# The up- and down-projection stages of a two-layer encoder: both down-projection units of a tile placed behind the third chain of sums

## The chip, the cores and the metric

The kernel runs on one core of a Trainium2 chip. The time is the device time of one execution in microseconds; a median of three executions is given, and one further execution was profiled. TensorE (PE in the profile) does the matrix products, with its weight loads shown apart as PEld; ScalarE (ACT) copies, casts and applies activation functions; VectorE (DVE) adds, subtracts and multiplies; GpSimd (POOL) and SyncE (SP) mostly issue transfers here.

## What is computed

The reference is a trunk of two layers on 512 tokens of width 1024. What matters here is the second half of each layer, the gated channel mixer with a causal convolution of width 3:

```python
def conv_ffn(h, w_up, conv_w, conv_b, w_down):
    u, g = jnp.split(h @ w_up, 2, axis=-1)
    g = causal_dwconv(g, conv_w, conv_b)
    return (jax.nn.silu(g) * u) @ w_down
...
x = x + conv_ffn(rmsnorm(x, norm_ffn_g[l]), ffn_w_up[l], ffn_conv_w[l], ffn_conv_b[l], ffn_w_down[l])
```

The hidden width is 2816, so the up-projection has 2 x 2816 columns (a part `u` and a part `g`), and the down-projection sums over 2816 rows. All of it is in float32.

## The kernel before

**Precision.** Every float32 operand is split into a high and a low part (`split`: a cast on ACT gives the high part, a subtraction on DVE the low one), and a product is three matmuls, high by high, high by low, low by high (`mm3`, lines 194 to 196). A chain is twelve such matmuls into one PSUM tile (four slices of the inner dimension).

**Tiles.** The mixer goes over 22 tiles `j` of 128 hidden columns. The first five (`plain`) are done as ordinary projections. Tiles 5 to 21 go through `later`, one call of `step` a tile; this loop runs once in each layer, and the change is inside `step`. There the `u` and `g` columns of a tile form a 2 x 2 block matrix whose product is taken with seven block products instead of eight (a Strassen-Winograd scheme). So a step has seven chains of matmuls 256 columns wide: a11, a12, s2, s1, s3, a22 and s4 in the order of the letters used below. The chains a11, s2, s3 and a22 add up in one PSUM tile `r1`, and after each of the four ACT copies the running sum out (`A.copy`, lines 842 and 834). The next chain into `r1` may not start before that copy is done. a12 goes to `r2`; s1 and s4 go to `r3`, whose half-way value DVE reads at line 857 before s4 may be added.

**Down-projection units.** The down-projection is cut into 32 units of twelve matmuls 512 columns wide (four hidden tiles into 128 output columns; `down_products`). A table `UNITS` says which units stand in which step: none in step 21, one in steps 5 to 8 (the second place), two in steps 9 to 20. I call the two places d0 and d1. After a unit, `add_down` copies its PSUM tile out on ACT (line 777) and a POOL transfer adds it to the sum in memory (line 778).

**Work for the neighbours.** Beside its own products a step finishes the tile before it (`Tail`: `last_block` at line 938, the convolution's taps at lines 692 and 685, Silu at line 950, the gate product at line 953, the split into hidden parts) and prepares the weights of the tile after it (`Forms`: sums and differences of weight blocks at line 888, and splits of them, each an ACT cast and a DVE subtraction at lines 140 and 141). `split_up`, `split_sums` and `split_down` split tiles of 1024 columns (into `wh`/`wl`), the others of 512 (into `fh`/`fl`).

**What sets the order.** Inside the loop PE, ACT and DVE run exactly in the order in which `step` is written (`manual_schedule`); each engine takes its instructions in order, so an instruction that waits holds up all that stands behind it on its engine. Loads on SP and transfers on POOL wait for buffers.

Of the kernel before, what the change touches and what calls it, by code (L numbers as in the profile page):

```python
# [46 lines left out]
H = S // 2  # L47
# [7 lines left out]
def trunk(  # L55
# [34 lines left out]
    def sb(tag, shape, dtype=F32):  # L90
        count[0] += 1
        return pool.tile(shape, dtype, tag=tag, name=f"{tag}{count[0]}", bufs=bufs[tag])

    def ps(tag):
        count[0] += 1
        return psum.tile([P, S], F32, tag=tag, name=f"p{tag}{count[0]}", bufs=pbufs[tag])
# [179 lines left out]
    class Norm:  # L276


        def __init__(self):
            self.acc = self.row = None  # L280
# [166 lines left out]
    with tc.manual_schedule(engines={mybir.EngineType.PE, mybir.EngineType.Activation, mybir.EngineType.DVE}):  # L447

        w = ps("mm")
# [215 lines left out]
    class ChannelMixer:  # L665
# [100 lines left out]
        def down_products(self, u):  # L766
            g, j = divmod(u, KT)
            w = self.down[u // 2]
            o = ps("tr")
            c = slice(u % 2 * P, (u % 2 + 1) * P)  # L770
            for k in range(GROUP):
                mm3(o, w[0][:, k, c], w[1][:, k, c], *self.hid[GROUP * g + k], k == 0, k == GROUP - 1)
            return j, o
# [52 lines left out]
        def step(self, j, w, nxt, tail):  # L826
            def then(o, *names):
                for name in names if o is not None else ():
                    getattr(o, name)()

            def sum_products(o, r, w, i):

                self.products(r, w, self.t(i))
                A.copy(o, r[:, :H])

            new = Tail(self, j)
            then(tail, "last_block", "first_tap")
            w.split_fourth()
            r1, r2, new.r3 = ps("mm"), ps("mm"), ps("sc")
            new.up, new.u3, new.pre = sb("t", [P, S]), sb("t", [P, S]), sb("t", [P, S])  # L840
            self.products(r1, w.a11, self.b(0, 0), True)
            A.copy(new.up[:, :H], r1[:, :H])
            then(tail, "second_tap")
            self.products(r2, w.a12, self.b(1, 0), True)
            V.tensor_tensor(out=new.up[:, :H], in0=new.up[:, :H], in1=r2[:, :H], op=ALU.add)
            then(tail, "third_tap")
            sum_products(new.up[:, H:], r1, w.s2, 2)
            then(nxt, "sums")
            then(tail, "gated")
            then(nxt, "split_second", "sum_third")  # L850
            w.down_products(0)
            self.products(new.r3, w.s1, self.t(1), True)
            w.add_down(0)
            then(tail, "split")
            then(nxt, "split_up")
            sum_products(new.u3[:, :H], r1, w.s3, 3)
            V.tensor_tensor(out=new.pre[:, H:], in0=new.u3[:, :H], in1=new.r3[:, :H], op=ALU.add)
            then(nxt, "split_sums")
            w.down_products(1)
            then(nxt, "sum_fourth")  # L860
            w.add_down(1)
            sum_products(new.pre[:, :H], r1, w.a22, 4)
            then(nxt, "split_down", "split_gate")
            self.products(new.r3, w.s4, self.b(1, 1))
            return new, nxt

    class Forms:


        def __init__(self, mixer, j):  # L870
            self.mixer = mixer
            self.units = UNITS.get(j, (None, None))
            self.up, self.gate = mixer.load_pair(j)
            self.raw_down = {u // 2: mixer.load_down(u // 2) for u in self.units if u is not None and u % 2 == 0}
            self.s13 = mixer.s[:, :D].rearrange("p (a b) -> p a b", a=KT)
            self.s24 = mixer.s[:, D : 2 * D].rearrange("p (a b) -> p a b", a=KT)
# [44 lines left out]

        def down_products(self, i):
            if self.units[i] is not None:
                self.o = self.mixer.down_products(self.units[i])

        def add_down(self, i):
            if self.units[i] is not None:
                self.mixer.add(*self.o)

    class Tail:  # L930

# [373 lines left out]
    def blocks(pt, o, step, n):  # L1305
        a = pt[:, o : o + P]
        return bass.AP(tensor=a.tensor, offset=a.offset, ap=[list(a.ap[0]), [step, n], [1, P]])
# [230 lines left out]
```

## Time and profile before

| | |
|---|---|
| median of 3 runs | 1180.85 us (1180.72 to 1180.89) |
| profiled execution, its own time | 1181.04 us |
| its span, first to last instruction | 1179.3 us |
| granted TensorE clock | 0.999 |
| one-unit step (steps 5 to 8), from one a11 to the next | about 12.3 us |
| two-unit step (steps 9 to 20) | about 15.0 us |

The page gives for each engine the time in which it was busy and its share of the span. Rows of a timeline start with the start time and the duration in microseconds; a bracket at the end gives the idle time of the engine before the instruction and what ended it. Rows of matmuls overlap, since matmuls are pipelined: what one costs is the distance from its start to the start of the next.

### The profile page before, as it was taken

How to read it: one execution, taken by the hardware profiler on the slowest of the kernel's cores; microseconds unless marked ns; L12 is line 12 of the kernel's file. 1: busy time of each engine (PE TensorE's matmuls, PEld its weight loads, DVE VectorE, ACT ScalarE, POOL GpSimd, SP SyncE). 2: the span in 40 equal slices, each digit the busy share in tenths (PEclk: the TensorE clock that was granted, in tenths of full speed). 3: DMA queues.
4: the chain of work that ended last, by engine and by line, in shares of the span. 5: the costliest groups of instructions: out<-in, count | busy, mean ns of one | idle time of the engine just before them, and what ended most of it. 6: DMA issues, size and time to landing. Idle time of an engine off the chain costs nothing.

```text
span 1179.3 us, 18676 instructions
## 1 busy us (share of the span) xinstructions
PE 1169.1 (99%) x7007; PEld 1034.2 (88%) x7007; DVE 935.7 (79%) x1688; ACT 725.8 (62%) x1294; POOL 129.9 (11%) x222
## 2 busy tenths in 40 slices
PE   9999999999999999999999999999999999999997
PEld 9988888888889999999888888888889999999986
DVE  6877788887978877777698888897897877777755
ACT  6548677654655655555666667776565655555545
POOL 1111101000021111111020000101001011111100
PEclk9999999999999999999999999999999999999999
DMA  8645325244266677765564312335426466666551
GB/s 299 208 109 134 94 55 152 76 139 121 90 166 163 164 164 162 164 148 129 150 200 125 90 54 85 106 102 177 139 90 153 108 143 144 143 143 141 123 158 72
DMA packets 200156, 158.64 MB, mean 135 GB/s; under 512 B 8344, under 2 KB 179838, under 8 KB 200066
## 3 DMA queue, kind: packets, MB, share of 16 engines
q1 hardware_dynamic: 183906, 119.74, 34.6%
q0 software_dynamic: 15584, 36.67, 16.4%
q8 instruction: 55, 0.90, 0.3%
q10 hardware_dynamic: 576, 1.05, 0.2%
q14 instruction: 35, 0.29, 0.1%
HBM read 128.89 MB, written 32.46 MB: 137 GB/s over the span
## 4 chain that ended last, share of the span: by engine, by line
PE 94%; DVE 3%; ACT 1%; issue 0%; DMA 0%; SPq 0%; POOL 0%; ACTq 0%; POOLq 0%; DVEq 0%
PE pmm L194 18%; PE pmm L195 18%; PE pmm L196 18%; PE ptr L195 6%; PE ptr L194 6%; PE ptr L196 6%; PE psc L195 5%; PE psc L196 5%; PE psc L194 5%; PE psc L544 2%; PE ptr L1365 1%; PE ptr L1386 1%; PE ptr L1387 1%; PE ptr L627 1%; PE ptr L613 0%; DVE pt L141 0%
## 5 line engine op out<-in xcount | busy, mean ns | idle before, releaser
L194 PE MATMUL pmm<-u,wh 128*128 128x512 f32 (+1 forms) x968 | 333.2, 345 | 0.4 <-ACT u L140 0.2
L196 PE MATMUL pmm<-u,wl 128*128 128x512 f32 (+1 forms) x968 | 330.8, 342 | 0.0
L195 PE MATMUL pmm<-u,wh 128*128 128x512 f32 (+1 forms) x968 | 330.5, 342 | 0.0
L141 DVE TENSOR_TENSOR wl<-wr,wh 128x1024 fp32r<-128x1024 f32 (+3 forms) x172 | 199.6, 1162 | 101.8 <-ACT wh L140 101.4
L140 ACT CAST wh<-wr 128x1024 fp32r<-128x1024 f32 (+3 forms) x172 | 172.0, 1002 | 92.7 <-PE pmm L195 39.0
L196 PEld LDWEIGHTS pmm<-u,wl 128*128 128x128 f32 x968 | 181.9, 188 | 20.6
L194 PEld LDWEIGHTS pmm<-u,wh 128*128 128x128 f32 x968 | 181.8, 188 | 19.3 <-ACT u L140 1.1
L195 PEld LDWEIGHTS pmm<-u,wh 128*128 128x128 f32 x968 | 182.0, 188 | 18.5 <-DVE u L141 0.5
L194 PE MATMUL ptr<-u,wh 128*128 128x512 f32 x272 | 106.7, 392 | 0.0
L195 PE MATMUL ptr<-u,wh 128*128 128x512 f32 x272 | 106.5, 392 | 0.0
L196 PE MATMUL ptr<-u,wl 128*128 128x512 f32 x272 | 105.8, 389 | 0.0
L778 POOL DMA_DIRECT2D xspill<-t x64 | 55.6, 869 | 447.3 <-ACT t L777 437.5
L141 DVE TENSOR_TENSOR fl<-pt,fh 128x512 fp32r<-128x512 f32 x102 | 70.3, 689 | 11.2 <-ACT fh L140 8.5
L194 PE MATMUL pmm<-u,fh 128*128 128x256 f32 x272 | 75.4, 277 | 0.0
L195 PE MATMUL pmm<-u,fh 128*128 128x256 f32 x272 | 75.2, 276 | 0.0
L196 PE MATMUL pmm<-u,fl 128*128 128x256 f32 x272 | 75.2, 276 | 0.0
L195 PE MATMUL psc<-u,wh 128*128 128x256 f32 (+1 forms) x232 | 75.1, 324 | 0.0
L196 PE MATMUL psc<-u,wl 128*128 128x256 f32 (+1 forms) x232 | 75.1, 324 | 0.0
L194 PE MATMUL psc<-u,wh 128*128 128x256 f32 (+1 forms) x232 | 75.0, 324 | 0.0
L140 ACT CAST fh<-pt 128x512 fp32r<-128x512 f32 x102 | 62.7, 615 | 13.5 <-DVE pt L888 13.3
L950 ACT ACTIVATE t<-t 128x512 f32<-128x512 f32 x34 | 21.5, 632 | 79.2 <-DVE t L685 79.2
L777 ACT COPY t<-ptr 128x512 f32<-128x512 f32 x64 | 37.6, 587 | 51.6 <-PE ptr L196 51.6
(335 smaller groups left out, 2540.3 us busy)
## 6 DMA issues: line engine op xcount, KB each, us to landing
wr<-in_ffn_w_up_dram SPq DMA_DIRECT2D x54, 512.0 KB, 5.0
wr<-in_ffn_w_down_dram SPq DMA_DIRECT2D x38, 512.0 KB, 4.1
pt<-in_ffn_w_up_dram SPq DMA_DIRECT2D x34, 512.0 KB, 6.9
xspill<-t POOLq DMA_DIRECT2D x64, 256.0 KB, 4.7
wr<-in_a_w_in_dram SPq DMA_DIRECT2D x20, 512.0 KB, 3.8
wr<-in_w_kv_dram SPq DMA_DIRECT2D x12, 512.0 KB, 4.0
xspill<-fh POOLq DMA_DIRECT2D x16, 256.0 KB, 2.6
xspill<-fl POOLq DMA_DIRECT2D x16, 256.0 KB, 3.0
```

Source lines behind the costliest of these rows:

```text
L140: high = A.copy(hi, src) if on_act else V.tensor_copy(hi, src)
L141: low = V.tensor_tensor(out=lo, in0=src, in1=f(hi), op=ALU.subtract)
L194: nc.tensor.matmul(o, lh, rh, start=first, stop=False, skip_group_check=more)
L195: nc.tensor.matmul(o, lh, rl, start=False, stop=False, skip_group_check=more)
L196: nc.tensor.matmul(o, ll, rh, start=False, stop=last, skip_group_check=more)
L544: nc.tensor.matmul(o, a, b, start=first and i == 0, stop=i == 1)
L627: nc.tensor.matmul(o2, vs[a][:, 2 * hp + h, :], p[h][:, a, :], start=i == 0, stop=i == 3)
L777: A.copy(t, o)
L778: G.dma_start(xspill[j], t, accum_op=ALU.add)
L950: A.activation(self.acc, self.acc, AF.Silu)
L1365: nc.tensor.transpose(tp[:, b * P : (b + 1) * P], es[T, h][:, b * P : (b + 1) * P], ident)
L1386: nc.tensor.matmul(o2[:, s * P :], w, hi_at(pts[h], s, s, TT - s), start=s == 0, stop=False)
```

## The change

Only the order inside `step` changes. On PE the chains of a two-unit step stood as a11, a12, s2, **d0**, s1, s3, **d1**, a22, s4; now they stand as a11, a12, s2, s1, s3, **d0, d1**, a22, s4. Since both units' PSUM tiles are now held at once, `self.o` becomes a dictionary with an entry for each. The ACT and DVE work is written in a new order around this:

```diff
-            then(tail, "second_tap")
+            then(tail, "second_tap", "third_tap")
             self.products(r2, w.a12, self.b(1, 0), True)
             V.tensor_tensor(out=new.up[:, :H], in0=new.up[:, :H], in1=r2[:, :H], op=ALU.add)
-            then(tail, "third_tap")
             sum_products(new.up[:, H:], r1, w.s2, 2)
             then(nxt, "sums")
+            self.products(new.r3, w.s1, self.t(1), True)
             then(tail, "gated")
             then(nxt, "split_second", "sum_third")
-            w.down_products(0)
-            self.products(new.r3, w.s1, self.t(1), True)
-            w.add_down(0)
+            sum_products(new.u3[:, :H], r1, w.s3, 3)
             then(tail, "split")
             then(nxt, "split_up")
-            sum_products(new.u3[:, :H], r1, w.s3, 3)
             V.tensor_tensor(out=new.pre[:, H:], in0=new.u3[:, :H], in1=new.r3[:, :H], op=ALU.add)
-            then(nxt, "split_sums")
+            w.down_products(0)
             w.down_products(1)
-            then(nxt, "sum_fourth")
+            then(nxt, "split_sums", "sum_fourth")
+            w.add_down(0)
+            then(nxt, "split_gate")
             w.add_down(1)
+            then(nxt, "split_down")
             sum_products(new.pre[:, :H], r1, w.a22, 4)
-            then(nxt, "split_down", "split_gate")
             self.products(new.r3, w.s4, self.b(1, 1))
...
-                self.o = self.mixer.down_products(self.units[i])
+                self.o[i] = self.mixer.down_products(self.units[i])
...
-                self.mixer.add(*self.o)
+                self.mixer.add(*self.o[i])
```

On PE, in step 12 of the first layer, the end of the unit d0 (`ptr891`) and what stands behind it, before: the chain s1 (`psc885`).

```order
L195 MATMUL ptr891_4770<-u786_4099,wh2874_4679 128x512
L196 MATMUL ptr891_4770<-u785_4098,wl2875_4680 128x512
L194 MATMUL psc885_4716<-u640_3275,wh1870_4645 128x256
L195 MATMUL psc885_4716<-u640_3275,wh1870_4645 128x256
L196 MATMUL psc885_4716<-u640_3275,wl1871_4646 128x256
```

The same place of the same step now: d0 is `ptr895`, and the second unit `ptr896` follows at once.

```order
L195 MATMUL ptr895_4804<-u785_4111,wh2876_4670 128x512
L196 MATMUL ptr895_4804<-u785_4111,wl2877_4671 128x512
L194 MATMUL ptr896_4817<-u680_3454,wh2876_4670 128x512
L195 MATMUL ptr896_4817<-u681_3455,wh2876_4670 128x512
L196 MATMUL ptr896_4817<-u680_3454,wl2877_4671 128x512
```

Between a unit and a chain of 256 columns PE now changes width twice in such a step, where it did so four times.

On ACT, from Silu of the tile before (line 950) to the last splits of the step, before. `t886` is the tile's `up`, `t887` its `u3`, `t888` its `pre`; `wh0` is `split_up`, `wh1` `split_sums`, `wh2` `split_down`, `fh889` `split_second`, `fh903` `split_gate`.

```order
L950 ACTIVATE t880_4708<-t880_4708 128x512
L834 COPY t886_4717<-pmm883_4714 128x256
L140 CAST fh889_4765<-pt633_3237 128x512
L777 COPY t892_4795<-ptr891_4770 128x512
L140 CAST u893_4798<-t880_4708 128x512
L140 CAST wh0895_4802<-wr878_4703 128x1024
L834 COPY t887_4718<-pmm883_4714 128x256
L140 CAST wh1897_4820<-pt633_3237 128x1024
L777 COPY t900_4838<-ptr899_4824 128x512
L834 COPY t888_4719<-pmm883_4714 128x256
L140 CAST wh2901_4854<-wr879_4705 128x1024
L140 CAST fh903_4858<-pt632_3236 128x512
```

The same stretch of ACT now (`fh900` is `split_gate`):

```order
L950 ACTIVATE t880_4708<-t880_4708 128x512
L834 COPY t886_4717<-pmm883_4714 128x256
L140 CAST fh889_4777<-pt633_3237 128x512
L834 COPY t887_4718<-pmm883_4714 128x256
L140 CAST u891_4795<-t880_4708 128x512
L140 CAST wh0893_4799<-wr878_4703 128x1024
L140 CAST wh1897_4830<-pt633_3237 128x1024
L777 COPY t899_4835<-ptr895_4804 128x512
L140 CAST fh900_4838<-pt632_3236 128x512
L777 COPY t902_4842<-ptr896_4817 128x512
L140 CAST wh2903_4845<-wr879_4705 128x1024
L834 COPY t888_4719<-pmm883_4714 128x256
```

The copy of `u3` has moved ahead of the casts of the hidden tile and of `split_up`; `split_gate` and `split_down` have moved ahead of the copy of `pre`.

On DVE, from `split_down` of the step before to the first sum of weight blocks, before:

```order
L141 TENSOR_TENSOR wl2875_4680<-wr852_4530,wh2874_4679 128x1024
L141 TENSOR_TENSOR fl877_4684<-pt632_3236,fh876_4683 128x512
L938 TENSOR_TENSOR t859_4542<-t859_4542,psc858_4541 128x256
L141 TENSOR_TENSOR fl882_4711<-pt633_3237,fh881_4710 128x512
L685 SCALAR_TENSOR_TENSOR t880_4708<-t861_4544,cols1_799,t880_4708 128x511
L845 TENSOR_TENSOR t886_4717<-t886_4717,pmm884_4715 128x256
L685 SCALAR_TENSOR_TENSOR t880_4708<-t861_4544,cols1_799,t880_4708 128x510
```

The same seven instructions now:

```order
L141 TENSOR_TENSOR fl874_4664<-pt632_3236,fh873_4663 128x512
L141 TENSOR_TENSOR wl2877_4671<-wr852_4530,wh2876_4670 128x1024
L938 TENSOR_TENSOR t859_4542<-t859_4542,psc858_4541 128x256
L141 TENSOR_TENSOR fl882_4711<-pt633_3237,fh881_4710 128x512
L685 SCALAR_TENSOR_TENSOR t880_4708<-t861_4544,cols1_799,t880_4708 128x511
L685 SCALAR_TENSOR_TENSOR t880_4708<-t861_4544,cols1_799,t880_4708 128x510
L845 TENSOR_TENSOR t886_4717<-t886_4717,pmm884_4715 128x256
```

`split_gate` and `split_down` have changed places, and the last tap (on which Silu waits) no longer stands behind the sum that reads a12's product.

More of the change, by code (lines that the diff above doesn't have):

```diff
@@ L873, in __init__ @@
             self.up, self.gate = mixer.load_pair(j)
+            self.o = {}
             self.raw_down = {u // 2: mixer.load_down(u // 2) for u in self.units if u is not None and u % 2 == 0}
```

## The prediction

> **What bounds the kernel now.** I read the page first, then busy time by stretch for the two loops that the change touches.
>
> ```profile
> span 1179.3 us, 18676 instructions
> PE 1169.1 (99%) x7007; PEld 1034.2 (88%) x7007; DVE 935.7 (79%) x1688; ACT 725.8 (62%) x1294; POOL 129.9 (11%) x222
> PE 94%; DVE 3%; ACT 1%; issue 0%; DMA 0%; SPq 0%; POOL 0%; ACTq 0%; POOLq 0%; DVEq 0%
> ```
> ```profile
> core 0: us, PE busy (x) PEld busy (x) DVE busy (x) ACT busy (x) POOL busy (x), PEclk, DMA share, GB/s
> 340.90:577.47 236.57, 236.52 (x1742) 222.60 (x1740) 186.57 (x273) 140.03 (x239) 39.51 (x53) 1.00 0.67 154
> 390.35:570.66 180.31, 180.31 (x1298) 168.55 (x1297) 141.44 (x206) 106.49 (x183) 29.79 (x39) 1.00 0.68 152
> 895.30:1132.00 236.70, 236.66 (x1742) 222.74 (x1741) 186.94 (x273) 140.46 (x240) 24.74 (x29) 1.00 0.62 139
> ```
>
> PE is busy throughout: 236.52 of 236.57 us in the first loop, 236.66 of 236.70 in the second, at full clock (1.00). DVE has 141.44 of 180.31 us of work in the twelve two-unit steps, ACT 106.49. So no wait of size can be removed, and PE's work is unchanged. Two small things are left to gain, and a new wait to lose. Since a busy PE may still be issuing late, I looked at distances between matmul starts.
>
> ```profile
> 331.16 0.39 PE L196 MATMUL ptr<-u,wl 128*128 128x512 f32 x1
> ...
> 339.32 0.39 PE L196 MATMUL ptr<-u,wl 128*128 128x512 f32 x1
> ...
> 390.35 0.28 PE L194 MATMUL pmm<-u,wh 128*128 128x256 f32 x1
> ...
> 495.53 0.28 PE L194 MATMUL pmm<-u,wh 128*128 128x256 f32 x1
> ...
> 499.61 0.40 PE L194 MATMUL ptr<-u,wh 128*128 128x512 f32 x1
> ...
> 570.66 0.28 PE L194 MATMUL pmm<-u,wh 128*128 128x256 f32 x1
> ```
>
> The first two rows are 36 matmuls apart, in tile 4, where units stand in a row with nothing between: 8.16 / 36 = 0.2267 us each, 2.72 a unit. From 495.53 (a11) to 499.61 (d0) are three chains of twelve, a11, a12, s2: 1.36 each. By these a two-unit step takes 7 x 1.36 + 2 x 2.72 = 14.96 us. It takes (570.66 - 390.35) / 12 = 15.026 (a11 of step 9 to a11 of step 21). The 0.066 left over belongs to two excursions from 256 columns to 512 and back, **0.033 us each**.
>
> One real stall stands in each loop, in step 7, between s1 and s3:
>
> ```profile
> 370.79 0.28 PE L196 MATMUL psc<-u,wl 128*128 128x256 f32 x1
> 371.11 0.38 PE L194 MATMUL pmm<-u,wh 128*128 128x256 f32 x1
> 371.33 0.28 PE L195 MATMUL pmm<-u,wh 128*128 128x256 f32 x1
> ...
> 925.17 0.28 PE L196 MATMUL psc<-u,wl 128*128 128x256 f32 x1
> 925.49 0.39 PE L194 MATMUL pmm<-u,wh 128*128 128x256 f32 x1
> 925.72 0.28 PE L195 MATMUL pmm<-u,wh 128*128 128x256 f32 x1
> ```
> ```profile
> 370.16 0.63 ACT L950 ACTIVATE t<-t 128x512 f32<-128x512 f32 x1 [2.53 <-DVE t L685]
> 370.70 0.35 ACT L834 COPY t<-pmm 128x256 f32<-128x256 f32 x1
> ```
>
> Two distances of 0.32 and 0.22 where 0.113 is normal: **0.32 us** lost, and in the second loop 0.32 + 0.23 likewise. s3 adds to the tile from which ACT copies s2's sum (370.70 to 371.05), and that copy stood behind Silu, which had waited 2.53 us for the last tap. s3 was due at 370.90. This shows the rule of the step: s2's copy has to be done when s3 is due, and Silu comes before it.
>
> **The change part by part.**
>
> *Both units together.* In each two-unit step one excursion goes: 12 steps x 2 layers x 0.033 = **-0.79 us**. That d1 behind d0 costs a plain 2.72 is shown by tile 4's units. Bounds: 0 (if the surcharge belongs to each unit after all) and 0.79. I take 0.79.
>
> [...]
>
> *Less cover for s2's copy.* Between s2 and s3 stood d0 and s1, 4.1 us; now s1 alone, 1.36. The same two-unit step at ACT and DVE:
>
> ```profile
> 493.00 0.59 ACT L777 COPY t<-ptr 128x512 f32<-128x512 f32 x1 [1.42 <-PE ptr L196]
> 494.37 0.37 ACT L834 COPY t<-pmm 128x256 f32<-128x256 f32 x1 [0.78 <-PE pmm L196]
> 494.64 1.05 ACT L140 CAST wh<-wr 128x1024 fp32r<-128x1024 f32 x1
> 495.60 0.61 ACT L140 CAST fh<-pt 128x512 fp32r<-128x512 f32 x1
> 496.11 0.81 ACT L692 ACTIVATE t<-t,cols 128x512 f32<-128x512 f32 x1
> 496.83 0.61 ACT L140 CAST fh<-pt 128x512 fp32r<-128x512 f32 x1
> ...
> 500.23 0.63 ACT L950 ACTIVATE t<-t 128x512 f32<-128x512 f32 x1 [2.53 <-DVE t L685]
> 500.77 0.35 ACT L834 COPY t<-pmm 128x256 f32<-128x256 f32 x1
> ```
> ```profile
> 492.75 0.69 DVE L888 TENSOR_TENSOR pt<-wr,pt 128x512 f32<-128x512 f32 x1
> 495.72 1.23 DVE L141 TENSOR_TENSOR wl<-wr,wh 128x1024 fp32r<-128x1024 f32 x1 [2.28 <-ACT wh L140]
> 496.87 0.69 DVE L141 TENSOR_TENSOR fl<-pt,fh 128x512 fp32r<-128x512 f32 x1
> 497.47 0.41 DVE L938 TENSOR_TENSOR t<-t,psc 128x256 f32<-128x256 f32 x1
> 497.80 0.68 DVE L141 TENSOR_TENSOR fl<-pt,fh 128x512 fp32r<-128x512 f32 x1
> 498.41 0.74 DVE L685 SCALAR_TENSOR_TENSOR t<-t,cols,t 128x511 f32<-128x511 f32 x1
> 499.40 0.74 DVE L685 SCALAR_TENSOR_TENSOR t<-t,cols,t 128x510 f32<-128x510 f32 x1
> ```
>
> As things stand the copy ends at 501.12, and s3 in its new place would be due at 495.53 + 4 x 1.36 = 500.97: 0.15 too late, just as in step 7. So all hangs on Silu coming earlier. I lay the same instructions out in the new order; PE's places around 495.53 stay. On one engine the next instruction starts about 0.1 before the printed end (495.60 + 0.61, then 496.11); between engines I add 0.03, and 0.20 from the next chain's start to a copy (s4 starts at 495.53 - 1.36 = 494.17, a22's copy at 494.37). The split of the down weights no longer waits for a22's copy: it follows d1's copy (493.00), cast 493.49 to 494.54. DVE, which idled 2.28 us here, has the gate split done by 494.1 and the down split at 494.57 to 495.80. ACT: pre's copy 494.45, first tap 494.72, cast for `split_fourth` 495.44 to 496.05. DVE: last block 495.73 (s4's end), `split_fourth` 496.08, taps 496.68 and 497.34 to 498.08, no longer around a12's sum. Silu starts at about **498.1 instead of 500.23**. s2's copy then waits for s2 alone, 499.81 to 500.18, and s3 has 0.8 us to spare. Cost **0**; with Silu where it is now, 0.32 a step.
>
> *s4 behind line 857.* The hidden cast and `split_up` now wait behind u3's copy, and DVE's half of `pre` behind them; s4 waits for it. That is tightest with one unit. Step 6 before:
>
> ```profile
> 360.69 0.36 ACT L834 COPY t<-pmm 128x256 f32<-128x256 f32 x1
> ```
> ```profile
> 362.21 0.41 DVE L857 TENSOR_TENSOR t<-t,psc 128x256 f32<-128x256 f32 x1
> ```
> ```profile
> 364.10 0.28 PE L194 MATMUL psc<-u,fh 128*128 128x256 f32 x1
> ```
>
> s3 ends at 364.10 - 1.36 - 2.75 = 359.99. New: u3's copy 360.19, hidden cast 360.46, `split_up` cast 360.98 to 362.03, its subtraction 362.06 to 363.28, then line 857 until 363.6. Due 364.10: 0.5 us to spare where there were 1.5. Two-unit steps have 2.7 more. Cost 0; if DVE is 0.9 late, 0.4 a step in steps 6 to 8.
>
> *Step 7.* I carry that layout on. DVE: `split_sums` 363.53 to 364.76, sum of the fourth form 364.67, gate split 365.27, down split 365.87 to 367.10, last block 367.01, `split_fourth` 367.33, taps 367.93 and 368.58 to 369.32. Silu 369.35 to 369.98, and s2's copy behind it 369.88 to 370.25, where it was 371.05; s3 is due at 370.90. **-0.32 x 2 = -0.64 us**; bounds 0 and -0.64.
>
> *The rest.* d0's copy and its transfer on POOL come 2.7 us later; nothing on PE waits for them until the sums are read back after the loop, whose last unit keeps its place. SP's loads wait for the down split, which ends 1.1 us earlier (495.80 against 496.95). Steps 5 to 8 and 21 keep PE's order. All 0.
>
> Sum: -0.79 - 0.64 = -1.43 us. The profiled execution took 1181.04 (span 1179.3, 1.7 around it); the median is 0.19 below it. **1180.85 - 1.43 = 1179.4 us.**
>
> **The rivals.**
>
> *The change of width is not what costs, or it is not saved.* For it: the surcharge was seen only as a remainder of 0.066 in 15. Against it: tile 4 has none. Only step 7 gains: 1180.85 - 0.64 = 1180.2. Chance 0.10. [...]
>
> *Step 7 keeps its stall.* Its margin is the smallest of the steps with a down split. 1180.85 - 0.79 = 1180.1, chance 0.12.
>
> *s2's copy becomes the wait of every two-unit step* (the slower side). One mechanism: Silu, ahead of the copy, starts after about 500.3 on the clock above, 2.2 us later than I laid out. For it: that is where it stands now, and step 7 has paid for it. Price 24 x 0.32 - 0.79 = +6.9, with step 7 kept: 1187.7. Half of the steps: 1183.9. Chance 0.12 for both.
>
> *s4 waits for line 857* in steps 6 to 8 of both layers: 6 x 0.4 = 2.4, less 1.43: 1181.8. Chance 0.06.
>
> *More is gained*, if starts come closer everywhere: nothing in the loops but the widths and step 7 is left to shrink, at most 0.79 more (the second excursion): 1178.6. Chance 0.06.
>
> **How the numbers follow.** My forecast has the rest, 0.54, and 1179.4 is its time. A difference below 0.2% (2.4 us) counts as none, about what a measurement of this kernel can tell. The forecast and the rivals at 1180.2, 1180.1, 1181.8 and 1178.6 all lie within it (0.88); the rival at 1183.9 to 1187.7 is slower (0.12). The layouts by hand are good to some tenths, so I keep 0.06 for faster, 0.81 for none and 0.13 for slower. The range from 1178.6 to 1181.7 holds all but the slower rivals.
>
> **What would show it.** Two-unit steps of 14.99 us from a11 to a11 (180.31 us for twelve becomes 179.9); d1 starting 2.75 after d0 and ending 2.72 later; no distance above 0.12 between s1 and s3 in step 7; Silu some 2 us earlier in the two-unit steps, ahead of s2's end, and ACT's copy of s2's sum released by PE rather than standing behind Silu. Wrong would be: s3 starting late in the two-unit steps with ACT's copy as releaser, s4 late with DVE at the sum into `pre`, or a time above 1183.

## The result, and the profile after

| | before | after |
|---|---|---|
| median of 22 runs each | 1180.96 us | 1179.48 us |
| ratio, 95% interval | | 0.9987 (0.9981 to 0.9993) |
| two-unit step, a11 to a11 | 15.026 us | 14.993 us |
| step 7, first layer, second layer | 12.61, 12.65 us | 12.27, 12.27 us |
| a11 of step 5 to a11 of step 21, first layer, second layer | 229.76, 229.80 us | 229.02, 229.02 us |

The kernel became 1.5 us faster. The interval is 0.8 to 2.2 us, so the gain is clear of the noise, but it is less than the 2.4 us (0.2%) below which the prediction counts a difference as none. The busy shares of the page hardly move:

```profile
span 1179.4 us, 18657 instructions
PE 1167.9 (99%) x7007; PEld 1033.9 (88%) x7007; DVE 941.3 (80%) x1688; ACT 730.0 (62%) x1294; POOL 129.7 (11%) x222
```

This span is no shorter than before's 1179.3, though the steps are. Most of the reason stands in the first microseconds, at the first transposes behind the first load. The timelines of PE show it for the kernel before, for the profiled run of after, and for after profiled once more:

```profile
6.24 0.66 PE L462 MATMUL psc<-ident,u 128*128 128x128 f32 x4 [0.45 <-DMA u<-in_mem_dram]
```
```profile
7.51 0.66 PE L462 MATMUL psc<-ident,u 128*128 128x128 f32 x4 [1.35 <-DMA u<-in_mem_dram]
```
```profile
6.09 0.73 PE L462 MATMUL psc<-ident,u 128*128 128x128 f32 x4
```

In the first profile of after, the transposes that wait for this load start 1.27 us later than before, and the loop began 1.71 later, at 342.61 instead of 340.90 (the other 0.44 was lost between the two, also ahead of the change). That execution took 1181.13 us, the slowest but two of its 22. The second profile of after begins the loop at 340.88, has the same steps, a span of 1177.7 and a time of 1179.39. So single executions differ by more than the change is worth, in places it doesn't touch, and only the lengths of steps and loops are compared below. By stretches, first the loop of before from a11 of step 5 to a11 of step 21, then the same of after and its twelve two-unit steps (columns as in the prediction):

```profile
340.90:570.66 229.76, 229.71 (x1681) 215.79 (x1680) 181.30 (x265) 136.34 (x233) 39.51 (x53) 1.00 0.67 152
```
```profile
342.61:571.63 229.02, 229.02 (x1682) 215.56 (x1680) 184.28 (x265) 138.97 (x234) 39.42 (x53) 1.00 0.65 152
391.71:571.63 179.92, 179.92 (x1299) 168.42 (x1297) 143.81 (x206) 108.16 (x182) 30.04 (x40) 1.00 0.64 152
```

The loop is 0.74 us shorter (0.78 in the second layer): 0.40 in the twelve steps, where 179.92 stands for 180.31, and the rest in step 7. PE's rows at the two places: s1's end and s3's start in step 7, then the first and the sixth matmul of d0 in a two-unit step, and the starts of d1, a22 and the next a11:

```profile
372.49 0.28 PE L196 MATMUL psc<-u,wl 128*128 128x256 f32 x1
372.60 0.28 PE L194 MATMUL pmm<-u,wh 128*128 128x256 f32 x1
372.71 0.28 PE L195 MATMUL pmm<-u,wh 128*128 128x256 f32 x1
...
488.47 0.40 PE L194 MATMUL ptr<-u,wh 128*128 128x512 f32 x1
...
489.63 0.39 PE L196 MATMUL ptr<-u,wl 128*128 128x512 f32 x1
...
491.21 0.39 PE L194 MATMUL ptr<-u,wh 128*128 128x512 f32 x1
...
493.93 0.28 PE L194 MATMUL pmm<-u,fh 128*128 128x256 f32 x1
...
496.66 0.28 PE L194 MATMUL pmm<-u,wh 128*128 128x256 f32 x1
```

d0 takes 2.74 and d1 behind it 2.72; in step 7 the distances are 0.11 throughout, where 0.32 and 0.22 stood. ACT in step 7 (two rows) and in the two-unit step, then DVE in the two-unit step:

```profile
371.27 0.63 ACT L950 ACTIVATE t<-t 128x512 f32<-128x512 f32 x1 [2.17 <-DVE t L685]
371.80 0.35 ACT L834 COPY t<-pmm 128x256 f32<-128x256 f32 x1
...
496.69 0.60 ACT L140 CAST fh<-pt 128x512 fp32r<-128x512 f32 x1
498.22 0.37 ACT L842 COPY t<-pmm 128x256 f32<-128x256 f32 x1 [0.92 <-PE pmm L196]
499.56 0.63 ACT L950 ACTIVATE t<-t 128x512 f32<-128x512 f32 x1 [0.97 <-DVE t L685]
500.94 0.38 ACT L834 COPY t<-pmm 128x256 f32<-128x256 f32 x1 [0.74 <-PE pmm L196]
```
```profile
495.70 1.23 DVE L141 TENSOR_TENSOR wl<-wr,wh 128x1024 fp32r<-128x1024 f32 x1 [1.26 <-ACT wh L140]
496.86 0.42 DVE L938 TENSOR_TENSOR t<-t,psc 128x256 f32<-128x256 f32 x1
497.33 0.69 DVE L141 TENSOR_TENSOR fl<-pt,fh 128x512 fp32r<-128x512 f32 x1
497.94 1.53 DVE L685 SCALAR_TENSOR_TENSOR t<-t,cols,t 128x511 f32<-128x511 f32 x2
```

To compare steps I count from a11 of the step ("+2.90" is 2.90 us after its start), and call **lead** the time from the end of the copy of s2's sum to the start of s3 in a step without a stall, which is +5.44 (four chains of 1.36). Silu stands at +2.90 here (499.56 against a11 at 496.66), where it stood at +4.70; the copy is released by PE and ends at +4.66, a lead of 0.78. In step 7 Silu is at +4.11, and the lead is 0.44. Step 9, the first with two units, follows a one-unit step and goes like step 7, not like the other two-unit steps (a11 at 391.71):

```profile
395.81 0.63 ACT L950 ACTIVATE t<-t 128x512 f32<-128x512 f32 x1 [2.17 <-DVE t L685]
396.35 0.36 ACT L834 COPY t<-pmm 128x256 f32<-128x256 f32 x1
```

Silu is at +4.11, the copy stands behind it, and the lead is 0.44; no time is lost by it.

### The profile page after: what moved, and what is told of

It reads as the page before. It is cut to its first block, busy times and chain, and to the rows that moved or that the text cites. A ratio compares the mean times of both kernels' runs of the same rounds, so it can differ in the third digit from the quotient of the medians.

```text
span 1179.4 us, 18657 instructions
## 1 busy us (share of the span) xinstructions
PE 1167.9 (99%) x7007; PEld 1033.9 (88%) x7007; DVE 941.3 (80%) x1688; ACT 730.0 (62%) x1294; POOL 129.7 (11%) x222
## 4 chain that ended last, share of the span: by engine, by line
PE 93%; DVE 3%; DMA 2%; ACT 1%; SPq 1%; issue 0%; POOL 0%; POOLq 0%; ACTq 0%; DVEq 0%
PE pmm L194 18%; PE pmm L195 18%; PE pmm L196 18%; PE ptr L195 6%; PE ptr L194 6%; PE ptr L196 6%; PE psc L196 5%; PE psc L195 5%; PE psc L194 5%; PE psc L544 2%; PE ptr L1365 1%; DMA wr<-in_mem_w_kv_dram 1%; PE ptr L1386 1%; PE ptr L1387 1%; DMA u<-in_mem_dram 1%; PE ptr L627 1%
## 5 line engine op out<-in xcount | busy, mean ns | idle before, releaser
L834 ACT COPY t<-pmm 128x256 f32<-128x256 f32 x102 | 38.2, 374 | 76.6 <-PE pmm L196 76.5
L141 DVE TENSOR_TENSOR u<-t,u 128x512 fp32r<-128x512 f32 (+1 forms) x94 | 54.3, 604 | 35.4 <-ACT u L140 35.4
```

Of the source, the lines that this page charges most:

```text
L141: low = V.tensor_tensor(out=lo, in0=src, in1=f(hi), op=ALU.subtract)
```

## The experiments

Each theory's numbers are those written before its run. Times of single executions are given, but the lengths of steps carry the verdicts.

**1. PE's new order alone.** The kernel before with d0 moved behind s3, and its copy behind d1 (it can't stand on ACT ahead of s3's copy there); all else on ACT and DVE as before.

```diff
-            w.down_products(0)
             self.products(new.r3, w.s1, self.t(1), True)
-            w.add_down(0)
...
+            w.down_products(0)
             w.down_products(1)
             then(nxt, "sum_fourth")
+            w.add_down(0)
             w.add_down(1)
```

> PE's new order with the ACT and DVE order of before (only d0's copy moves, behind d1). Theory (the earlier Silu is what keeps s3 from waiting): Silu starts about 4.7 us after a11 as it did before, the copy of s2's sum ends about 5.6 us after a11, s3 is due at 5.44, so each of the 24 two-unit steps loses about 0.32 us between s1 and s3, and step 7 keeps its 0.32: 24 x 0.32 = +7.7, less 0.8 for the widths, on 1181.0 gives about 1187.9 us (1186 to 1189). Rival (s1 alone is cover enough, the ACT and DVE order does nothing): no such waits, about 1180.2 us.

Measured: 1188.48 us, ratio to before 1.0062 (1.0049 to 1.0076). Its twelve two-unit steps, and ACT, PE and the weight loads (PEld) where s3 begins in one of them (a11 at 421.54):

```profile
390.84:574.92 184.08, 183.53 (x1299) 169.68 (x1297) 138.16 (x206) 106.27 (x183) 29.81 (x39) 1.00 0.64 150
```
```profile
426.25 0.63 ACT L951 ACTIVATE t<-t 128x512 f32<-128x512 f32 x1 [2.53 <-DVE t L685]
426.79 0.35 ACT L834 COPY t<-pmm 128x256 f32<-128x256 f32 x1
```
```profile
426.87 0.28 PE L196 MATMUL psc<-u,wl 128*128 128x256 f32 x1
427.19 0.39 PE L194 MATMUL pmm<-u,wh 128*128 128x256 f32 x1
427.42 0.28 PE L195 MATMUL pmm<-u,wh 128*128 128x256 f32 x1
```
```profile
427.19 0.19 PEld L194 LDWEIGHTS pmm<-u,wh 128*128 128x128 f32 x1 [0.24 <-ACT t L834]
```

Silu is at +4.70 as before (426.25 waits for the last tap), the copy ends at +5.60, and s3 starts 0.32 behind the matmul ahead of it in every two-unit step, just as in step 7 before. Most of these steps take 15.33 us, 0.34 more than after's; the extremes are 15.31 and 15.38. So the other half of the change, the new order on ACT and DVE, is what lets the new order on PE gain at all. The row of the weight load shows where the wait for ACT stands in these kernels: at the load of the weights, not at the matmul behind it.

**2. The last tap alone.** The kernel before with the last tap ahead of a12's sum.

```diff
-            then(tail, "second_tap")
+            then(tail, "second_tap", "third_tap")
...
-            then(tail, "third_tap")
```

> The kernel before with one edit: the last tap stands ahead of the sum that reads a12. Theory: in step 7 Silu comes 0.33 us earlier, the copy of s2's sum ends at about 370.72 where s3 is due at 370.90, so the stall goes or falls under 0.1 us in both loops; two-unit steps stay at 15.026 us; 1181.0 - 0.6 = about 1180.4 us. Rival (the stall went because the down split moved ahead of the copy of pre): step 7 still loses 0.2 us or more, about 1180.9 us.

Measured: 1180.69 us, ratio 0.9996 (0.9987 to 1.0005). Step 7 takes 12.447 us: 0.17 is left of the stall, so the number fell between the two expectations. DVE, ACT, PE and weight loads there (a11 at 365.19):

```profile
368.07 1.53 DVE L685 SCALAR_TENSOR_TENSOR t<-t,cols,t 128x511 f32<-128x511 f32 x2
```
```profile
369.69 0.63 ACT L949 ACTIVATE t<-t 128x512 f32<-128x512 f32 x1 [2.32 <-DVE t L685]
370.23 0.35 ACT L834 COPY t<-pmm 128x256 f32<-128x256 f32 x1
```
```profile
370.52 0.28 PE L196 MATMUL psc<-u,wl 128*128 128x256 f32 x1
370.64 0.39 PE L194 MATMUL pmm<-u,wh 128*128 128x256 f32 x1
370.86 0.28 PE L195 MATMUL pmm<-u,wh 128*128 128x256 f32 x1
```
```profile
370.41 0.19 PEld L196 LDWEIGHTS psc<-u,wl 128*128 128x128 f32 x1
370.63 0.19 PEld L194 LDWEIGHTS pmm<-u,wh 128*128 128x128 f32 x1
370.74 0.19 PEld L195 LDWEIGHTS pmm<-u,wh 128*128 128x128 f32 x1
```

Two things are read here. Silu came 0.20 earlier (+4.50), not by the 0.33 that the sum between the taps had taken: the two taps in a row take 1.53 for 2 x 0.74, so here the second starts only when the first is done. And s3 loses 0.17 although the copy (to 370.58) ended 0.05 before s3 was due at 370.63. The load of s3's first weights started at 370.63, 0.05 after the copy's end, where it would have followed the load before it by 0.11, at 370.52.

**3. More changes of width.** Each unit cut into two halves of six matmuls, behind a12, s2, s1 and s3, with the taps and splits in after's order: four excursions to 512 columns in a two-unit step, and two in a one-unit step.

```diff
+            w.half(0, 0)
             sum_products(new.up[:, H:], r1, w.s2, 2)
             then(nxt, "sums")
+            w.half(0, 1)
...
+            w.half(1, 0)
             sum_products(new.u3[:, :H], r1, w.s3, 3)
             V.tensor_tensor(out=new.pre[:, H:], in0=new.u3[:, :H], in1=new.r3[:, :H], op=ALU.add)
+            w.half(1, 1)
```

> Each unit is cut into two halves of six matmuls, and the four halves stand apart between chains of 256 columns, so a two-unit step has four excursions to 512 columns and back; same work, taps and splits ordered as in the changed kernel. Theory (0.033 us an excursion): two-unit step 14.96 + 4 x 0.033 = 15.09 us, no waits at s3, 1181.0 + 24 x 0.066 - 0.64 = about 1181.9 us. Rival (the surcharge belongs to a unit, not to a change of width): two-unit step 15.03 us, about 1180.3 us.

Measured: 1182.15 us, ratio 1.0010 (1.0001 to 1.0019). The twelve two-unit steps:

```profile
391.21:572.33 181.12, 181.12 (x1299) 168.80 (x1297) 141.24 (x204) 107.13 (x181) 29.89 (x39) 1.00 0.70 151
```

181.12 / 12 = 15.093 a step. With the same matmuls, one excursion gives 14.993, two 15.026, four 15.093: 0.033 each. Nothing waits (PE is busy for all of it). The expectation left out the one-unit steps: they also became 0.033 longer (12.307), 0.27 us over the kernel, which with 24 x 0.067 = 1.6 makes 1.9, less the 0.7 of the stall in step 7 that this order takes away too: 1.2; the medians differ by 1.25.

**4. The last tap put back.** After, with the last tap behind a12's sum again.

```diff
-            then(tail, "second_tap", "third_tap")
+            then(tail, "second_tap")
...
+            then(tail, "third_tap")
```

> The changed kernel with the last tap put back behind the sum that reads a12. Theory: Silu starts about 1.2 us later in the two-unit steps (from 2.9 to about 4.1 us after a11), the copy ends about 5.0 us after a11, s3 due at 5.44 doesn't wait; in step 7 the margin of 0.4 us shrinks to under 0.1, a loss of at most 0.15 us a loop. Two-unit steps stay at 14.99 us, time about 1179.6 us. Rival (the tap's place is what carries the whole change): s3 loses 0.2 us or more in each two-unit step, 15.2 us a step, about 1184 us.

Measured: 1179.48 us (one run), 14.993 a step and 12.273 in step 7, whose lead fell to 0.24. In the two-unit steps Silu is at +4.17, since the tap now waits for a12 through the sum, and the lead is 0.38. One step of the second layer took 15.13 (step 12, a11 at 988.45):

```profile
992.90 0.63 ACT L951 ACTIVATE t<-t 128x512 f32<-128x512 f32 x1 [2.51 <-DVE t L685]
993.44 0.35 ACT L834 COPY t<-pmm 128x256 f32<-128x256 f32 x1
```
```profile
993.67 0.19 PEld L196 LDWEIGHTS psc<-u,wl 128*128 128x128 f32 x1
993.84 0.19 PEld L194 LDWEIGHTS pmm<-u,wh 128*128 128x128 f32 x1
```

Its tap ended at 992.52; Silu followed 0.38 later, where 0.10 is usual, for a reason that the trace doesn't show. It is no accident of this run: in the same step of the second layer Silu comes 0.28 late in both profiles of after too (+3.18 instead of +2.90), where it costs nothing, since the copy waits for s2. The copy ended at 993.79, the load of s3's weights again 0.05 after it at 993.84, and 0.14 was lost at a lead of 0.10.

**5. The split of the down weights put back** behind the copy of `pre`, in after.

```diff
-            then(nxt, "split_down")
             sum_products(new.pre[:, :H], r1, w.a22, 4)
+            then(nxt, "split_down")
```

> The changed kernel with the down split put back behind the copy of pre (the gate split stays ahead of both). Theory: what counts for Silu is the DVE work ahead of the taps, and the down split's DVE part is the same length in either place, so Silu moves by under 1 us in the two-unit steps (from 2.9 to about 3.7 us after a11), the copy still waits for s2 alone, no loss at s3 anywhere, two-unit steps 14.99 us, steps 6 to 8 12.27 us. Rival (it is the earlier down split that made Silu early): Silu at 4 us or later, step 7 loses 0.1 us or more again.

Measured: 1179.62 us (one run); in the two-unit steps behind step 9 Silu is at +3.89 (409.03, a11 at 405.14), the lead 0.66; all steps are as long as in after.

**6. Both put back.** The edits of 4 and 5 together, so that of the new order on ACT and DVE there remain above all the gate split ahead of the down split, and the copy of `u3` ahead of the hidden cast.

> The changed kernel with both the last tap and the down split back in their old places; of the ACT and DVE order only the gate split ahead of the down split and the early copy of u3 are left. Theory (the gate split's 0.6 us of DVE, no longer between the down split and the taps, is enough): Silu about 4.0 us after a11 in the two-unit steps, the copy ends some 0.5 us before s3 is due, no loss: 14.99 us a step; step 7 loses at most 0.15. About 1179.6 us. Rival (tap and down split are needed, as in the run with the old ACT and DVE order): 0.3 us a two-unit step, 15.3 us, about 1187 us.

Measured: 1179.63 us (one run); Silu at +4.16 (409.25, a11 at 405.09), lead 0.38, two-unit steps of 14.993 (again one of 15.13, the same step as in 4); in step 7 lead 0.24 and 12.273, no loss, where up to 0.15 had been allowed.

**7. The gate split alone.** The kernel before with `split_gate` ahead of d1's copy, and so ahead of the down split.

```diff
-            then(nxt, "sum_fourth")
+            then(nxt, "sum_fourth", "split_gate")
             w.add_down(1)
             sum_products(new.pre[:, :H], r1, w.a22, 4)
-            then(nxt, "split_down", "split_gate")
+            then(nxt, "split_down")
```

> The kernel before with one edit: the gate split moves ahead of the copy of d1 and so ahead of the down split. Theory: in step 7 Silu and the copy of s2's sum come 0.6 us earlier, 0.4 us ahead of s3's due time, and the stall of 0.32 us goes in both loops (step 7 from 12.59 to 12.27 us); two-unit steps keep their 15.026 us; about 1180.3 us. Rival (the tap or the down split has to move too): step 7 keeps 0.1 us or more of its stall.

Measured: 1180.66 us beside 1180.59 of before, one run each, which tells nothing of 0.3 us. The steps do: the loop is 229.42 long instead of 229.76, and step 7 12.273. ACT there (a11 at 365.89):

```profile
370.05 0.63 ACT L950 ACTIVATE t<-t 128x512 f32<-128x512 f32 x1 [2.23 <-DVE t L685]
370.59 0.35 ACT L834 COPY t<-pmm 128x256 f32<-128x256 f32 x1
```

Silu is at +4.17, 0.53 earlier, and the stall is gone whole at a lead of 0.38. Where the time came from shows on DVE, at the down split in step 7 of before and of this kernel:

```profile
365.65 1.23 DVE L141 TENSOR_TENSOR wl<-wr,wh 128x1024 fp32r<-128x1024 f32 x1 [1.29 <-ACT wh L140]
366.79 0.69 DVE L141 TENSOR_TENSOR fl<-pt,fh 128x512 fp32r<-128x512 f32 x1
367.40 0.41 DVE L938 TENSOR_TENSOR t<-t,psc 128x256 f32<-128x256 f32 x1
```
```profile
366.08 1.23 DVE L141 TENSOR_TENSOR wl<-wr,wh 128x1024 fp32r<-128x1024 f32 x1 [0.69 <-ACT wh L140]
367.22 0.41 DVE L938 TENSOR_TENSOR t<-t,psc 128x256 f32<-128x256 f32 x1
```

The down split starts at +0.19 in both. The gate split (366.79) is gone from behind it, and the wait ahead of it is 0.60 shorter, since the gate split now stands in it.

**8. After once more**, for its late start.

> The changed kernel once more, for a second profile. Theory: its first profile's span of 1179.4 us holds a late start of about 1.7 us ahead of the first layer's loop (TensorE's first matmuls), which has nothing to do with the change; the same stretches of the two loops show 14.993 us a two-unit step and 12.273 us in step 7 again, and a span near 1177.8 us if the start is as in the other profiles. Rival (the change itself made the start late): the start is late again and the span 1179.4 us.

Measured: 1179.39 us, span 1177.7, steps as in the first profile; its rows stand with the result.

The runs on one scale, lead of s2's copy and what s3 lost by it:

| kernel and place | lead, us | lost, us |
|---|---|---|
| PE's order alone, two-unit steps | -0.16 | 0.32 to 0.39 |
| before, step 7 | -0.15 | 0.34, 0.38 |
| last tap alone, step 7 | 0.05 | 0.17 |
| tap put back, both put back, one step | 0.10 | 0.14 |
| tap put back, both put back, step 7 | 0.24 | 0 |
| gate split alone, step 7 | 0.38 | 0 |
| after, steps 7 and 9; steps 10 to 20 | 0.44; 0.78 | 0 |

## Why the prediction was right, point by point

*Both units together, -0.79.* Right in mechanism and size: 12 x 2 x 0.0333 = 0.80. That a change of width costs, and not a unit as such, was the open point; experiment 3 settles it, since its steps have the same two units' worth of matmuls as before and after. The rival without a saving is out: three steps of the same matmuls are 14.993, 15.026 and 15.093 long. Nor is it a change of the PSUM tile that costs, since d1 behind d0 changes the tile at a plain 2.72. The Trainium skill, "TensorE: Matmul & The Clock Gate", section "Back-to-back issue gap", gives a gap by the columns alone only for an isolated matmul, N / 2.4 + 2.5 ns when warm (215.8 ns at 512 columns, 109.2 at 256). For a stream of weight loads and matmuls it says that both set the spacing, and gives about 131 ns at 512 columns; the matmuls here are such a stream, and the trace doesn't agree: they stand 226.7 ns apart (2.72 us / 12).

*Step 7, -0.64.* Right in mechanism. The size was 0.34 + 0.38 = 0.72: I counted the two long distances, but some matmuls behind them stood 0.12 apart instead of 0.113 until s3 had caught its pace. With this the loops gained 0.74 + 0.78 = 1.52 where 1.43 was predicted. That the medians moved by 1.48, within 0.05 of the forecast, is in part luck, since their interval is 1.4 us wide; the loops carry the agreement.

*Less cover for s2's copy, 0.* Right, and the layout by hand held where it mattered: 0.8 us to spare was predicted, and 0.78 measured in steps 10 to 20. I had laid out only these and step 7. In step 9 Silu still sets the copy, at a lead of 0.44, so step 7 isn't alone with the smallest margin. Silu itself was laid out at +2.57 and came at +2.90. The rows above show most of the 0.33: the cast for `split_fourth` ended at 497.29 and held its subtraction (497.33) 0.12 longer than I had laid out; the two taps take 1.53, not 1.40 (0.66 from the one's start to the other's and 0.74); and Silu followed their end at 499.47 by 0.09, not 0.03. It cost nothing in steps 10 to 20, because the copy of s2's sum waits for s2. In step 7, where Silu sets the copy, the same things took the lead from the predicted 0.65 to 0.44.

*The rule of the step* was a little wrong. I let the copy be done when s3 is due. In these kernels it has to be done some 0.16 earlier: the load of s3's first weights stands 0.11 ahead of its matmul and is the one that waits, and it starts 0.05 after the copy's end. By it the losses in the table begin between leads of 0.10 and 0.24, which the runs bracket. With the predicted margins this decided nothing.

*Why Silu came earlier.* I laid the new order out whole and didn't say which edit does it. The one that is enough in step 7 is the gate split, 0.6 us of DVE that stood behind the down split and ahead of the taps: moved ahead of it, it falls into the time in which DVE waits for ACT's cast (experiment 7). Alone it gives 0.53 and removes the stall there; the tap and the earlier down split together without it weren't run. The rest of the 1.80 takes the tap and the earlier down split together, since with either put back Silu is at +4.17 or +3.89; it buys lead only. Both can go back at no loss but the 0.14 of one step (experiment 6). That the gate split is also enough for PE's new order isn't quite shown: experiment 6 also keeps the earlier copy of `u3`, which no run took out by itself.

*s4 behind line 857.* 0.5 us to spare in step 6 was predicted; the row of the sum (line 854 now) and s4, due at 365.80:

```profile
364.90 0.42 DVE L854 TENSOR_TENSOR t<-t,psc 128x256 f32<-128x256 f32 x1
```

It ends at 365.32, 0.48 ahead. The rival that s4 waits is out.

*The slower rival*, s2's copy as the wait of every two-unit step, didn't come, but its mechanism is real: with Silu left at +4.70 (experiment 1) the price was mostly 0.34 a step where the rival had 0.32, and the time 1188.48 where it had 1187.7.

*The rest.* The signs named beforehand are there: steps of 14.99 us, 179.92 for twelve, d1 2.74 behind d0 and 2.72 long, no distance above 0.12 in step 7 and, in steps 10 to 20, Silu 1.8 us earlier (some 2 were named) and the copy released by PE. In step 9 the last two are missing: Silu is 0.6 us earlier, and the copy stands behind it. The loops' 1.52, the 1.48 between the medians and the 1.6 between the spans of before and of after's second profile agree within some tenths, so nothing of size was gained or lost outside the loops.

What stays open: why an excursion costs 0.033 (most of it lies in d0's first five matmuls, which take 489.63 - 488.47 = 1.16 where five of 0.227 are 1.13; a22 behind the units takes a little over 1.36), and why Silu comes 0.28 late in step 12 of the second layer, in after and in experiments 4 to 6. Taking away the one excursion left in each two-unit step, 0.8 us in all, wasn't tried.

## What to carry to other kernels

Before a chain is moved closer to one that adds to the same PSUM tile, lay out what stands ahead of the copy between them on the copying engine: here the same move on PE made the kernel 7.6 us slower with Silu where it was, and the whole change, with Silu out of the way, 1.5 us faster. The edit that removed the stall was the one that moved 0.6 us of work from behind a long wait into it; the tap, nearest to the late instruction, took away only half of it. Where gains are tenths of a microsecond, compare steps and loops of the trace: a start that came 1.7 us later, 1.3 of it at one input load, hid the whole gain in one profile.

## What the runs showed of the hardware

- **Here a copy out of PSUM had to end before the weight load of the next chain's first matmul, not before that matmul.** The loads of s3's first weights started 0.05 us after the copy's end in three kernels (427.19, 370.63, 993.84), and a lead of 0.05 to 0.10 us still cost 0.14 to 0.17. That is where the wait for ACT stands in the trace; no run here had it at the matmul, so nothing shows that PSUM itself asks for it.
- **A change of width on PE cost 0.033 us there and back** between matmuls of 256 and 512 columns, the same for one, two and four excursions in a step (14.993, 15.026 and 15.093 us).
- **The two taps, of which the second reads what the first writes, didn't overlap on DVE.** Other instructions there start 0.07 us before the printed end of the one ahead (495.70 + 1.23, then 496.86); the taps took 1.53 us for 2 x 0.74, so taking the sum from between them brought Silu forward by 0.20 us, not by the 0.33 that it takes up in a row of others.
